# Three changes of place in a hybrid decoder block: the pools of a rows stage, the first loads of the attention mix, and the tiles of the second feed-forward product

## The chip, the cores and the metric

The kernel runs on one core of a Trainium2 chip. The metric is the time of one execution in microseconds of the device. The time before is the median of three runs. One execution was recorded by the hardware profiler, and all lines of a profile come from it. The engines are PE (matrix products), DVE, ACT and POOL (vector work), and SP, which here issues most of the DMAs (POOL issues the stores made with `store`).

## The reference, cut to what matters

One layer on x of 2048 rows by 1024 columns, all in float32:

```python
h = rmsnorm(x, norm_pre_mix)
z = h @ w_in                      # columns: g_u g_v | f_q f_k f_v | f_gate | m_q
out_a = gmlp_spatial_gating(g_u, g_v, w_s, b_s, v_norm)      # 6 groups x 64, chunks of 128
out_b = forgetting_attention(f_q, f_k, f_v, log_sigmoid(f_gate + b_forget))   # 6 heads x 64, causal
out_c = memory_cross_attention(m_q, rmsnorm(mem), w_mem_kv)  # 4 heads x 64, 256 memory rows
x = x + rmsnorm(concat(out_a, out_b, out_c) @ w_out)
f = square(relu(rmsnorm(x) @ w_ff1)) @ w_ff2                 # 1024 -> 4096 -> 1024
x = x + rmsnorm(f)
```

## The kernel before, in words

**Numbers and products.** Every product is made from three matmuls: each operand is split into a high part (a rounded copy, ACT, L195, or `halves` at L399 to L403) and a low part (the difference, mostly DVE, L197), and high x high, high x low and low x high are added in PSUM (`mm3`, L203 to L205). The large products use seven products of blocks in place of eight. Their numbers 1, 7, 2, 6, 4, 5, 3 are in the names of the tiles: m = 7, 5, 6 and 3 are sums and differences of blocks, made by POOL or DVE, the others are blocks themselves. A product of a stage is `product(acc, m, first)`.

**Stages.** The 2048 rows are two halves, s = 0 and 1, of 1024 rows.

1. `rows_stage(s, h)`: loads pairs of 128-row tiles of x (L411), norms them, transposes them on PE (`pt`, L431), makes the halves and the block sums of h, stores h for later use to `bq_d` (L444), and multiplies by the value columns (`va`). The values go to `v_d` (L457) and the forget gates to `gate`. Its SBUF pools are xa, xb, xd, xv and xc, opened in that order, for normed rows, block sums, values, and high and low halves. They are closed at the end of the stage, and the next stage's weight pools take their addresses.
2. The columns stage (`column_weights`, `columns`): the rest of w_in, in column blocks. Raw weights `wr0c`, `wr1c` are loaded, their sums `sc` made, split into `w_c`, and used in the products `fxc`, `fyc`, `fzc`. Results go through split copies (`oh_c`, `ol_c`) to `qhi`, `qlo`, `khi`, `klo` and others in device memory. After the second rows stage `forget_sums` (L476 on) makes the cumulative log-sigmoid; it needs an Exp table on ACT.
3. The attention mix: the scores, softmax and value products of every head (L825, L826, L836, L865, L745 to L767), the gating (`gating`), the memory heads and the output weights' loads are steps of a planner (`Plan`), each with an engine, a cost and an earliest time. Its run gives the order in which instructions are written on every engine. `loads` and `block` in `forgetting` issue the loads of q, of the keys, of the cumulative sums (`cb`) and of the values; `tokens` in `gating` issues the loads of a tile of h (`hr`, two DMAs from `bq_d`), which ACT casts to `ht` and POOL completes, for the gating products `ga`.
4. The output product, its norm, and the norm and block sums for the feed-forward part.
5. The first feed-forward product: for each s, 16 blocks `pr` of 256 columns of w_ff1. Per block POOL makes four sums of weights (`sf`, L289 to L292), ACT and DVE split seven blocks of weights, PE runs seven products, and relu and square on ACT (L1429, L1430) write `hid`, 512 x 512 tiles in device memory. POOL also makes one sum of products per block (`c_f`, L322), which waits for product 5's neighbour `k_f` on ACT. `last_chunk(pr)`, in s = 1 only, does ahead of time what the last chunk of the second product needs: for each of eight units u it loads hidden values (`lr`) at block LATER[u], makes four sums on POOL (`ls`, L1368 to L1371) one block later, and splits them (`lh`) and stores them to `hs_d` (L1401) two blocks later.
6. The second feed-forward product: eight chunks c of 512 rows of w_ff2, each with four pairs of units (s, n, q). `chunk_weights(c)` loads two pieces `w2r` (L1472), makes their eight sums on POOL (L1476 to L1479) and splits them into `w`; `unit` loads the hidden values `hr` (L1504), makes four sums `hs` (`hidden_sums`, L1368 to L1371) and splits them into `hc`. The products `gx`, `gy`, `gz` are added into `ya` in SBUF (L1523, L1525). The loads of the first pieces `w2r0` are issued only after the load of block 10 of w_ff1 (`issue_after(loads["f1_10"])`).

**What sets the order.** Outside the mix, instructions are written in the order in which a scheduler places the code, and the pools decide what a new tile waits for: a tile at an address that earlier tiles used can only be written when their last readers are done. Code in `tc.high_priority()` is placed ahead; `behind(ins)` holds it until an instruction is placed. DMAs of SP leave in the order of its queue, and a wait in SP holds everything behind it.

**Places in SBUF at the boundary of 5 and 6.** `extra` (pool `wox`, on the right side) holds one raw block of the output weights and of s = 0's hidden input, and stays open to the end of the first product. `h2raw` (right) is the raw tile for s = 1's input. After it, before the change, lr (2 tiles), ls (8) and lh (7) are all opened on the right. When the first product ends, `ff_st` closes, and the second product opens its pools, `fraw` for the raw pieces `w2r` among them.

## Time and profile before

| what | value |
| --- | --- |
| time, median of three runs | 2284.72 us (2282.15 to 2287.16) |
| the profiled execution's own time | 2283.18 us |
| its span | 2281.1 us |
| mean granted clock of PE | 0.983 |
| busy: PE, DVE, ACT, POOL | 2173.9, 1632.0, 1354.7, 1029.2 us |
| rows stage s=1 (140 to 192.5): PE busy | 47.74 of 52.50 us |
| attention mix (297 to 833): PE busy | 501.01 of 536.00 us |
| first feed-forward product (1010 to 1640): PE busy | 617.80 of 630.00 us |
| boundary (1640 to 1660): PE busy | 12.40 of 20.00 us |
| second product (1660 to 2255): PE busy | 595.00 of 595.00 us |

A timeline line gives the start, the time of one instruction or of a group (x2, x4), the engine, the line of the kernel, the operation, output <- input, and in brackets the idle time before it with what ended it. The granted clock is the share of full speed that PE's clock had; at 0.50 a matmul takes twice its time.

### The profile page before, as it was taken

The page shows a single profiled execution, that of the slowest core. Times are in us where ns is not written, and L with a number is a line of the kernel's source. Part 1 is how long each engine was busy: PE and PEld are TensorE (multiplying, and loading weights), DVE is VectorE, ACT ScalarE, POOL GpSimd, SP SyncE. Part 2 cuts the span into 40 slices and gives each one's busy share as a digit, 9 for nine tenths or more (in the row PEclk, how much of TensorE's full clock was granted, in tenths as well). Part 3 has the DMA queues.
Part 4 walks back from the last instruction along what each step waited for, and adds up shares of the span by engine and source line. Part 5 has one row for each costly group of instructions (what it writes and reads, how often), then busy time and mean ns, then how long its engine had stood idle before and what let it go on. Part 6 is the DMA issues. An engine that isn't in the chain of part 4 may idle for free. (4 is left out here: it accounts for less than half of the span.)

```text
span 2281.1 us, 33146 instructions
## 1 busy us (share of the span) xinstructions
PE 2173.9 (95%) x10468; PEld 1827.3 (80%) x10468; DVE 1632.0 (72%) x3137; ACT 1354.7 (59%) x2929; POOL 1029.2 (45%) x1073
## 2 busy tenths in 40 slices
PE   8998989999999989998999999999899999999997
PEld 7787778888888867776888878888778888888885
DVE  7776657777877788895333364555678988999888
ACT  6465467878777776665555576666554443444333
POOL 5444433452636255644333334444655345534524
PEclk9999999999999989999999999999999999999998
DMA  7775685365463255785333364555432212221277
GB/s 253 248 241 173 211 226 139 84 165 135 104 153 98 83 180 204 262 293 203 111 111 111 111 212 152 194 193 184 151 111 93 93 56 93 93 92 57 93 248 296
DMA packets 236843, 359.98 MB, mean 158 GB/s; under 512 B 24806, under 2 KB 141420, under 8 KB 235644
## 3 DMA queue, kind: packets, MB, share of 16 engines
q1 hardware_dynamic: 224380, 316.92, 44.1%
q0 software_dynamic: 12288, 40.95, 4.8%
q8 instruction: 83, 1.36, 0.2%
q14 instruction: 92, 0.75, 0.1%
HBM read 232.88 MB, written 124.91 MB: 157 GB/s over the span
## 5 line engine op out<-in xcount | busy, mean ns | idle before, releaser
L205 PE MATMUL fxf<-h,w_f 128*128 128x512 f32 x512 | 201.3, 393 | 4.1 <-DVE w_f L197 4.1
L203 PE MATMUL gx<-w,hc 128*128 128x512 f32 x512 | 199.0, 391 | 6.4 <-DVE ya L1525 5.8
L204 PE MATMUL fxf<-h,w_f 128*128 128x512 f32 x512 | 200.9, 392 | 2.4 <-DVE h L197 2.4
L203 PE MATMUL fxf<-h,w_f 128*128 128x512 f32 x512 | 201.1, 393 | 1.1 <-ACT k_f L317 0.6
L195 ACT ACTIVATE hc<-hs 128x256 fp32r<-128x256 f32 x224 | 93.4, 417 | 179.6 <-PE gx L205 99.2
L204 PE MATMUL gx<-w,hc 128*128 128x512 f32 x512 | 199.7, 390 | 0.0
L205 PE MATMUL gx<-w,hc 128*128 128x512 f32 x512 | 196.4, 390 | 0.0
L197 DVE TENSOR_TENSOR w_f<-sf,w_f 128x512 fp32r<-128x512 f32 x128 | 95.9, 750 | 138.3 <-ACT w_f L195 135.9
L1525 DVE TENSOR_TENSOR ya<-gx,ya 128x512 f32<-128x512 f32 x232 | 156.6, 684 | 43.9 <-PE gx L205 43.2
L753 DVE TENSOR_TENSOR pl<-pt,ph 128x512 fp32r<-128x512 f32 x240 | 140.9, 605 | 46.9 <-ACT ph L749 45.4
L865 ACT ACTIVATE p<-p,nm 128x512 f32<-128x512 f32 (+2 forms) x240 | 156.9, 657 | 24.6 <-DVE nm L855 24.3
L749 ACT CAST ph<-pt 128x512 fp32r<-128x512 f32 x240 | 120.5, 523 | 62.5 <-PE pt L745 55.5
L195 ACT ACTIVATE w_f<-sf 128x512 fp32r<-128x512 f32 x128 | 80.8, 631 | 100.4 <-PE fxf L204 56.9
L197 DVE TENSOR_TENSOR w_f<-wrf,w_f 128x512 fp32r<-128x512 f32 x96 | 75.6, 788 | 88.2 <-ACT w_f L195 88.2
L836 DVE CUSTOM_DVE_ANT_0 p<-s,cb 128x512 f32<-128x512 f32 (+2 forms) x216 | 124.7, 593 | 17.6 <-PE pt L745 9.7
L197 DVE TENSOR_TENSOR hc<-hs,hc 128x256 fp32r<-128x256 f32 x224 | 124.9, 560 | 9.3 <-ACT hc L195 9.1
L195 ACT ACTIVATE hc<-hr 128x256 fp32r<-128x256 f32 x168 | 68.3, 416 | 101.4 <-PE gx L205 64.8
L745 PE MATMUL pt<-ident,p 128*128 128x128 f32 x816 | 123.9, 277 | 2.7 <-ACT p L865 2.7
L815 POOL TENSOR_TENSOR cm<-cb,cmask 128x128 f32<-128x128 f32 x96 | 45.0, 469 | 175.2 <-DVE mx L836 141.5
L745 PEld LDWEIGHTS pt<-ident,p 128*128 128x128 f32 x816 | 102.7, 144 | 22.9 <-ACT p L865 2.9
L203 PEld LDWEIGHTS gx<-w,hc 128*128 128x128 f32 x512 | 96.3, 188 | 28.4 <-DVE ya L1525 7.4
L205 PEld LDWEIGHTS fxf<-h,w_f 128*128 128x128 f32 x512 | 97.1, 190 | 26.0 <-DVE w_f L197 5.7
(389 smaller groups left out, 7066.8 us busy)
## 6 DMA issues: line engine op xcount, KB each, us to landing
wrf<-in_w_ff_dram SPq DMA_DIRECT2D x64, 512.0 KB, 4.8
hid<-c_f SPq DMA_DIRECT2D x128, 256.0 KB, 2.5
hr<-hid SPq DMA_DIRECT2D x56, 512.0 KB, 4.0
w2r<-in_w_ff_dram SPq DMA_DIRECT2D x16, 1024.0 KB, 5.6
b<-ty POOLq DMA_DIRECT2D x56, 256.0 KB, 3.8
hs<-lh SPq DMA_DIRECT2D x56, 256.0 KB, 2.7
hc<-hs SPq DMA_DIRECT2D x56, 256.0 KB, 5.1
xt<-in_x_dram SPq DMA_DIRECT2D x16, 512.0 KB, 4.7
```

The costliest lines, as they stand in the source:

```text
L195: a = nc.scalar.activation(hi, src, AF.Copy, scale=scale)
L197: return a, (eng or nc.vector).tensor_tensor(out=lo, in0=src, in1=f32(hi), op=ALU.subtract)
L203: nc.tensor.matmul(acc, lh, rh, start=first, stop=False, skip_group_check=more)
L204: nc.tensor.matmul(acc, lh, rl, start=False, stop=False, skip_group_check=more)
L205: nc.tensor.matmul(acc, ll, rh, start=False, stop=last, skip_group_check=more)
L745: nc.tensor.transpose(pt[:, a * P : (a + 1) * P], source(a, j), ident)
L749: nc.scalar.copy(hi[:, a0 * P :], tiles["pt", j][:, a0 * P :])
L753: nc.vector.tensor_tensor(out=lo[:, a0 * P :], in0=tiles["pt", j][:, a0 * P :], in1=f32(tiles["hi", j][:, a0 * P :]), op=ALU.subtract,)
L815: nc.gpsimd.tensor_tensor(out=t["cm", i], in0=cc[b][:, qs], in1=cmask, op=ALU.add)
L836: nc.vector.tensor_tensor_reduce(out=pr[:, cols], in0=t["s", a, c][:, cols], in1=sub, scale=1.0, scalar=-3.0e38, op0=ALU.subtract, op1=ALU ...
L865: nc.scalar.activation(pr, pr, AF.Exp, bias=t["nm", a], accum_out=t["rs"][:, a, c : c + 1])
L1525: nc.vector.tensor_tensor(out=y, in0=a, in1=y, op=ALU.add)
```

## The change

Three things are moved. No instruction is added or taken away.

**A, pools of the rows stage.** The pools are opened in the order xa, xd, xc, xb, xv. The sum of their sizes stays, but the weight tiles of the columns stage behind them lie where xd and xc were rather than where xb was.

**B, the start of the mix.** The tile for the gating's tokens is taken where it was, but its two loads are put into a list `held`. They are issued at once only if a key has been loaded already; otherwise when `block` has issued its loads (`token_loads` at its end). The first tile's loads are put behind the first key's second half.

**C, the second product's places.** `extra` is closed after the raw tile of s = 1; `fraw` is opened in its place, before the first product of s = 1 runs; ls has 4 tiles on the left in place of 8 on the right; lh and lr stay on the right. The units of the last chunk are taken from block 0 on.

```diff
@@ rows_stage
             xa = st.enter_context(pool(f"xa{s}", 1))
+            xd = st.enter_context(pool(f"xd{s}", 1))
+            xc = st.enter_context(pool(f"xc{s}", 2))
             xb = st.enter_context(pool(f"xb{s}", 6))
-            xd = st.enter_context(pool(f"xd{s}", 1))
             xv = st.enter_context(pool(f"xv{s}", 4))
-            xc = st.enter_context(pool(f"xc{s}", 2))
@@ load_pair
-            load(t[HD:, :n], lo[r, cols])
+            loads[tag] = nc.sync.dma_start(f32(t[HD:, :n]), lo[r, cols])
@@ forgetting, block
                     load(vv[c], v_d[4 * c : 4 * c + 4, :, h, :].rearrange("i p d -> p i d"))
+                    token_loads()
@@ ahead of gating
+        held = []
+
+        def token_loads():
+
+            while held:
+                t, i = held.pop(0)
+                s, e, q = i // 8, i // 4 % 2, i % 4
+                with behind(*[loads["k"]][: i < 1]):
+                    for k2 in range(2):
+                        nc.sync.dma_start(t[:, k2 * KH : (k2 + 1) * KH], bq_d[s][q][:, ((1, 2), (0, 3))[e][k2]])
@@ gating, tokens
-                        s, e, q = i // 8, i // 4 % 2, i % 4
                         t["hr", i] = xp.tile([P, D], F32, name=f"hr{i}", tag="x").rearrange("p (k t) -> p k t", k=KT)
-                        for k2 in range(2):
-                            nc.sync.dma_start(
-                                t["hr", i][:, k2 * KH : (k2 + 1) * KH], bq_d[s][q][:, ((1, 2), (0, 3))[e][k2]]
-                            )
+                        held.append((t["hr", i], i))
+                        if "k" in loads:
+                            token_loads()
@@ feed-forward part
-    extra = ff_st.enter_context(pool("wox", 1, side="right")), "x"
+    extra_st, down_st = ExitStack(), ExitStack()
+    extra = extra_st.enter_context(pool("wox", 1, side="right")), "x"
...
-        lp, LATER = {}, (1, 3, 4, 6, 7, 9, 10, 12)
+        lp, LATER = {}, (0, 1, 2, 4, 5, 6, 8, 9)
...
-                lp.update({a: st.enter_context(pool(f"l{a}", n, side="right")) for a, n in (("r", 2), ("s", 8), ("h", 7))})
+                extra_st.close()
+                down_raw = down_st.enter_context(pool("fraw", 2, side="right"))
+                lp["s"] = st.enter_context(pool("ls", 4))
+                lp.update({a: st.enter_context(pool(f"l{a}", n, side="right")) for a, n in (("h", 7), ("r", 2))})
...
-    with ExitStack() as st:
+    with down_st as st:
...
-        rp = st.enter_context(pool("fraw", 2, side="right"))
+        rp = down_raw
```

Three places show how the order moves. The first is ACT at the end of the second rows stage, before (-) and after (+): `vs` are the last two values, `w_c` the first column weights' high parts, `ls` the forget sums.

```order
 L195 ACTIVATE vs_2046<-va_2021 128x6x64
 L195 ACTIVATE vs_2076<-va_2051 128x6x64
-L476 ACT_TABLE_LOAD
-L476 ACTIVATE ls<-ls 128x96
 L195 ACTIVATE w_c_0_1_2115<-wr0c_0_2098 128x512
 L195 ACTIVATE w_c_0_7_2133<-sc_0_7_2104 128x512
 L195 ACTIVATE w_c_0_2_2151<-wr1c_0_2099 128x512
 L195 ACTIVATE w_c_0_6_2175<-sc_0_6_2106 128x512
+L476 ACT_TABLE_LOAD
+L476 ACTIVATE ls<-ls 128x96
```

The table load and the Exp of the forget sums moved behind four splits.

The second is SP at the start of the attention mix, first before the change. `cb` is a row of cumulative sums, `hr` the gating's tokens, `v`, `q` and `k` a head's values, queries and keys.

```order
L802 DMA cb_0_3126<-c_d 128x512
L1052 DMA hr_3112<-bq_91 128x512 x2
L189 DMA v_0_3128<-v_d 128x4x128
L802 DMA cb_1_3133<-c_d 128x512
L189 DMA q_0_1_3115<-qhi_67 64x512 x2
L189 DMA q_0_1_3118<-qlo_70 64x512 x2
L189 DMA k_0_3123<-khi_73 64x512
L189 DMA k_0_3123<-klo_76 64x512
```

The same place after the change:

```order
L802 DMA cb_0_3124<-c_d 128x512
L189 DMA v_0_3126<-v_d 128x4x128
L802 DMA cb_1_3133<-c_d 128x512
L189 DMA v_1_3135<-v_d 128x4x128
L802 DMA cb_2_3227<-c_d 128x512
L189 DMA q_0_1_3113<-qhi_67 64x512
L699 DMA q_0_1_3113<-qhi_67 64x512
L189 DMA q_0_1_3116<-qlo_70 64x512
L699 DMA q_0_1_3116<-qlo_70 64x512
L189 DMA k_0_3121<-khi_73 64x512
L699 DMA k_0_3121<-klo_76 64x512
L986 DMA hr_3112<-bq_91 128x512 x2
```

The tokens' two loads moved behind the first key, and one more tile of values and one more row of sums came ahead of it.

The third is POOL in block 12 of the first product in s = 1, where block 13's weight sums `sf` are made; `ls` are sums for the last chunk, `c_f_12` is block 12's sum of products. Before:

```order
L1368 TENSOR_TENSOR ls_7_17252<-lr_17069 128x256
L1369 TENSOR_TENSOR ls_5_17253<-lr_17069 128x256
L289 TENSOR_TENSOR sf_13_7_17446<-wrf_13_17443 128x512
L1370 TENSOR_TENSOR ls_6_17254<-ls_5_17253,lr_17069 128x256
L1371 TENSOR_TENSOR ls_3_17255<-lr_17069,ls_6_17254 128x256
L290 TENSOR_TENSOR sf_13_5_17447<-wrf_13_17443 128x512
L291 TENSOR_TENSOR sf_13_6_17448<-sf_13_5_17447,wrf_13_17443 128x512
L292 TENSOR_TENSOR sf_13_3_17449<-wrf_13_17443,sf_13_6_17448 128x512
L322 TENSOR_TENSOR c_f_12_17404<-k_f_12_17402,k_f_12_17324 128x512
```

And after; L1490 to L1493 are the lines L1476 to L1479 of before, the sums of the first rows of w_ff2:

```order
L1490 TENSOR_TENSOR t_0_7_18031<-w2r_0_18029 128x512
L1490 TENSOR_TENSOR t_1_7_18040<-w2r_1_18038 128x512
L290 TENSOR_TENSOR sf_13_5_17487<-wrf_13_17483 128x512
L1491 TENSOR_TENSOR w2r_0_18029<-w2r_0_18029 128x512
L1491 TENSOR_TENSOR w2r_1_18038<-w2r_1_18038 128x512
L1492 TENSOR_TENSOR t_0_6_18032<-w2r_0_18029 128x512
L291 TENSOR_TENSOR sf_13_6_17488<-sf_13_5_17487,wrf_13_17483 128x512
L1492 TENSOR_TENSOR t_1_6_18041<-w2r_1_18038 128x512
L1493 TENSOR_TENSOR t_0_4_18033<-w2r_0_18029,t_0_6_18032 128x512
L292 TENSOR_TENSOR sf_13_3_17489<-wrf_13_17483,sf_13_6_17488 128x512
L1493 TENSOR_TENSOR t_1_4_18042<-w2r_1_18038,t_1_6_18041 128x512
L322 TENSOR_TENSOR c_f_12_17474<-k_f_12_17472,k_f_12_17394 128x512
```

The eight sums of w2r moved here from the boundary, where they stood behind block 14's `c_f` and among the first `hs` sums; the `ls` sums of unit 6 are gone from this block.

## Prediction

> **What bounds the kernel now.** I read the windows first, then the timelines of the engines around each stretch that the change touches. The page's first line gives the span.
>
> ```profile
> span 2281.1 us, 33146 instructions
> ```
>
> The profiled execution took 2283.18 us, 2.1 more than this span and 1.5 less than the median of 2284.72. My sum is made against 2283.18, and 1.5 is added at the end. The windows below have as columns: length, then busy time and count for PE, PEld, DVE, ACT and POOL, then granted clock, DMA share, GB/s.
>
> ```profile
> 179.50:182.50 3.00, 1.44 (x7) 1.47 (x8) 3.00 (x6) 2.01 (x4) 2.80 (x3) 0.66 0.77 191
> 197.50:200.90 3.40, 3.40 (x9) 2.57 (x9) 3.40 (x7) 0.75 (x2) 1.37 (x1) 0.50 1.10 326
> 299.90:303.30 3.40, 3.11 (x9) 2.42 (x10) 1.64 (x7) 0.65 (x2) 3.34 (x4) 0.50 1.07 343
> 310.10:313.50 3.40, 2.79 (x8) 2.55 (x9) 1.59 (x6) 2.85 (x7) 1.09 (x1) 0.51 1.06 244
> 1566.04:1585.08 19.04, 19.04 (x86) 15.77 (x85) 13.55 (x17) 12.99 (x27) 10.43 (x9) 1.00 0.70 234
> 1640.00:1660.00 20.00, 12.40 (x43) 8.83 (x42) 17.19 (x21) 11.12 (x24) 13.86 (x12) 0.83 0.09 21
> 1644.80:1651.60 6.80, 4.23 (x10) 3.37 (x11) 6.80 (x6) 2.15 (x5) 6.64 (x7) 0.50 0.09 34
> 1660.00:2255.00 595.00, 595.00 (x2626) 492.34 (x2625) 527.60 (x933) 247.71 (x573) 287.07 (x294) 1.00 0.35 119
> ```
>
> The last row says that in the second product PE never waits: 595.00 of 595.00 at full clock. Over most of the program PE is the bound, and the same matmuls are issued before and after. So time can only be won where PE stands idle, and in the half-clock stretches behind such idle time: a stretch of 3.4 us at 0.50 does 1.7 us of full-clock work and costs 1.7. The change touches three such places: the end of the second rows stage (180 to 197), the start of the attention mix (297 to 311), and the boundary between the two feed-forward products (1640 to 1660). A gain there should stay, because PE is full behind it and the later order is unchanged. Differences under 0.2%, or 4.6 us, can hardly be told from no change.
>
> **Part A, the pools of the rows stage.** The same tiles get other addresses, and the next stage's column weights no longer wait for the same readers. In stage s=0 no engine's order changes, so I cost it at nothing. In s=1 PE has these idle times:
>
> ```profile
> 178.85 0.63 PE L431 MATMUL pt<-ident,h 128*128 128x128 f32 x4 [1.13 <-DVE h L399]
> 181.06 1.30 PE L431 MATMUL pt<-ident,h 128*128 128x128 f32 x5 [1.58 <-DVE h L399]
> ...
> 196.74 0.50 PE L203 MATMUL fxc<-hc,w_c 128*128 128x512 f32 x1 [4.24 <-ACT w_c L195]
> ```
>
> The last one waits for ACT's split of the first column weights. On ACT that split stands behind the table load of the forget gate:
>
> ```profile
> 192.54 0.87 ACT L195 ACTIVATE vs<-va 128x384 fp32r<-128x384 f32 x2 [0.94 <-PE va L205]
> 194.59 1.28 ACT L476 ACT_TABLE_LOAD   x1 [1.18 <-issue]
> 195.89 0.28 ACT L476 ACTIVATE ls<-ls 128x96 f32<-128x96 f32 x1
> 196.08 0.61 ACT L195 ACTIVATE w_c<-wr0c 128x512 fp32r<-128x512 f32 x1
> ```
>
> After the change four w_c splits stand directly behind the two vs splits, and the table load behind them. ACT is free of vs at 192.54 + 0.87 = 193.41. Today PE starts 196.74 - 196.08 = 0.66 after the split starts, so it would start at about 194.07: 2.67 us earlier, with an idle time of 4.24 - 2.67 = 1.57 left. What is late next is DVE's low half of the same weights: it now stands ahead of the L477 to L481 chain instead of behind its start, so it is not late. The forget sums move back by four splits. Nothing at the start of the columns stage reads them.
>
> The two idle times at L431 wait for DVE's normalised rows. The tiles' loads move ahead of two stores in SP's queue, and the L399 steps move forward in DVE's order. The most that can go is 1.13 + 1.58 and one half-clock stretch, 4.4 in all. On the other side DVE was busy for the whole of the 3.00 us in the first row of the windows, so moving one step forward moves another back, and the second half of the last weight load now stands behind a store of v_d: I allow a loss of 1.6, one more wait of the longer kind. Because of the full DVE I take 1.3, nearer to nothing than to 4.4. I leave the half-clock stretch at 197.5 where it is, since an idle time of 1.57 remains. Part A: 2.7 + 1.3 = 4.0, from 1.1 to 7.1.
>
> [...]
>
> **Part B, the first keys ahead of the gating's tokens.** PE waits twice here:
>
> ```profile
> 300.19 0.77 PE L825 MATMUL s<-k,q 128*128 128x512 f32 x1 [3.46 <-DMA k<-klo]
> ...
> 310.71 0.77 PE L826 MATMUL s<-k,q 128*128 128x512 f32 x1 [3.19 <-DMA q<-qlo]
> ```
>
> SP issues the loads:
>
> ```profile
> 285.07 0.35 SPq L802 DMA_DIRECT2D cb<-c_d  x1
> 287.83 0.80 SPq L1052 DMA_DIRECT2D hr<-bq  x2
> ...
> 294.08 0.55 SPq L189 DMA_DIRECT2D k<-klo  x1
> ...
> 305.10 0.45 SPq L189 DMA_DIRECT2D q<-qlo  x1
> ```
>
> Before the tokens (hr) SP stands still from 285.42 to 287.83, 2.41 us, until their buffer is free. The first key's second half is issued at 294.08. After the change the tokens go behind the first key, so this stop no longer delays it. But v_1 and cb_2 come ahead of it instead: two transfers of the tokens' size, so the bytes ahead of the key stay the same. The gain at the first wait lies between 0 and 2.41, and I take 1.5: the stop of 2.41 is wholly behind the key in the new order, but four q loads still come first. The second wait ends 310.71 - 305.10 = 5.6 us after the last q load's issue. That load still stands behind the gating weights and four wur loads. PE reaches it 1.5 earlier and waits longer there, up to the whole 1.5. I count half of that back: net 0.7.
>
> The moved tokens are two DMAs. Issued behind the key, at about 294.08 - 1.5 + 0.55 = 293.1, they land by the same 5.6 at 298.7. Work of the scores stands between that and the first gating products on PE. If that cover is gone, ACT waits at the tokens' cast with the first exponentials queued behind it: up to 2 us lost. Part B: 0.7, from -2 to 3. The upper end is the 2.41 and part of the second wait.
>
> **Part C, the places for the second product.** The boundary costs 20.00 - 12.40 = 7.60 us of idle PE, and from 1644.8 PE ran 4.23 us at half clock, 2.1 lost: about 9.7 in all.
>
> ```profile
> 1642.63 0.47 PE L203 MATMUL gy<-w,hc 128*128 128x512 f32 x1 [1.42 <-DVE c_f L322]
> 1642.93 0.40 PE L204 MATMUL gy<-w,hc 128*128 128x512 f32 x1
> 1647.37 0.79 PE L205 MATMUL gy<-w,hc 128*128 128x512 f32 x1 [4.04 <-DVE hc L197]
> ```
>
> Both waits are for DVE, and DVE is slow because POOL works beside it:
>
> ```profile
> 1637.25 2.94 DVE L197 TENSOR_TENSOR w<-w2r,w 128x512 fp32r<-128x512 f32 x2
> 1640.11 1.77 DVE L197 TENSOR_TENSOR w<-t,w 128x512 fp32r<-128x512 f32 x1
> 1641.80 0.68 DVE L322 TENSOR_TENSOR c_f<-fyf,k_f 128x512 f32<-128x512 f32 x1
> 1642.40 0.68 DVE L197 TENSOR_TENSOR w<-t,w 128x512 fp32r<-128x512 f32 x1
> 1643.00 2.90 DVE L197 TENSOR_TENSOR hc<-hr,hc 128x256 fp32r<-128x256 f32 x2
> 1645.83 1.49 DVE L197 TENSOR_TENSOR hc<-hs,hc 128x256 fp32r<-128x256 f32 x1
> ```
>
> The same split of w took 0.68 and 1.77. POOL at that time:
>
> ```profile
> 1632.69 3.00 POOL L1477 TENSOR_TENSOR w2r<-w2r 128x512 f32<-128x512 f32 x2
> 1636.04 0.74 POOL L1368 TENSOR_TENSOR hs<-hr 128x256 f32<-128x256 f32 x1 [0.36 <-DMA hr<-hid]
> 1636.74 1.19 POOL L1369 TENSOR_TENSOR hs<-hr 128x256 f32<-128x256 f32 x1
> 1637.89 3.44 POOL L1478 TENSOR_TENSOR t<-w2r 128x512 f32<-128x512 f32 x2
> ```
>
> After the change w_ff2's first rows are loaded some blocks earlier and their eight sums (L1476 to L1479) stand among block 13's weight sums, away from the boundary. The hidden loads are issued earlier too. DVE's eight steps from 1637.25 to 1647.32 take 10.07 us. At 0.68 each, the price without POOL and an upper one for the 256-wide steps, they take 5.4: at most 4.6 saved. But POOL still has two units of four hidden sums there, whose first waits for PE to give its buffer free, so it cannot move ahead. If each holds a DVE step up by 1.19 - 0.68 = 0.5, that is 4.0 of the 4.6, leaving 0.6. Between these ends I take 3 for the wait of 4.04, because the hidden sums come early in that stretch, and 1 of the 1.42. Nothing of the half-clock loss is counted. Part C: 4.0. Its upper end is 7 (the two waits whole, 5.5, and most of the half-clock loss), its lower end -1: the last sum of block 15 (c_f on POOL) now stands behind ten hidden sums, and its relu on ACT ahead of a split of w that PE needs. Ten sums at 0.74 to 1.19 are 7.4 to 11.9 us, so that chain may end a little after PE's need.
>
> At block 12 the eight sums use POOL's idle time, 19.04 - 10.43 = 8.6 us there, and the four ls sums that move away. Spare POOL time is the cover that makes them free. The second rival prices its loss. The earlier places of the LATER splits are steps of equal number among other blocks with PE full: nothing.
>
> **Sum.** 4.0 + 0.7 + 4.0 = 8.7 us: 2283.18 - 8.7 = 2274.5, and 1.5 more on the scale of the median, 2276.0. All lower ends together (1.1 - 2 - 1) give 2286.6, all upper ends (7.1 + 3 + 7) 2267.6.
>
> **Rivals.** First, the waits are given back: B's second wait takes all of the first, and the new chain POOL c_f, ACT relu, w split takes C's place. Then only A's 2.7 stays, 2282.0. For it: both second waits are in the rows above or in the order. Against it: the eight POOL sums do leave the boundary. Chance 0.20, within 0.2%.
>
> Second, slower: POOL is overfull in block 12.
>
> ```profile
> 1586.44 0.63 ACT L1429 ACTIVATE c_f<-c_f 128x512 f32<-128x512 f32 x1 [1.12 <-POOL c_f L322]
> ```
>
> ACT already waits here for POOL's last sum of the block, with the next splits behind it. Eight sums at 1.50 to 1.72 are 12.0 to 13.8. The four ls sums that leave have at most the row's mean of 10.43 / 9 = 1.16 each, at least half of it: 2.3 to 4.6. So 7.4 to 11.5 come into 8.6 of idle time: it fits, or is 2.9 over. Each sum can also hold DVE up by 1.77 - 0.68 = 1.09, 8.7 together, against DVE's idle 19.04 - 13.55 = 5.5: 3.2 over. A product is 19.04 / 7 = 2.7 us of PE, and the split behind c_f is for a product about three later, so it decides when lateness exceeds roughly 5 us. If both overruns reach PE (6.1) with two half-clock stretches (3.4), A and B's 4.7 are outweighed, and if C gives nothing as well the time is 2284.7 + 4.8 = 2289.5, or 2290. Against it: mostly it fits, and three products cover the rest. Chance 0.08.
>
> Third, more: the clock stays up behind the shortened idle times. Then the stretches at 197.5 and at 310.1 or 299.9 stay full, 2 x 1.7 = 3.4 more: 2272.6. [...] The 0.66 beside 1.13 and 1.58 speaks against it. Chance 0.10.
>
> **How the numbers follow.** The forecast has 0.62, between its own ends mostly 2268 to 2280. Faster: 0.62 + 0.10 = 0.72; within 0.2%: 0.20; slower: 0.08. The range from 2268 to 2286 takes in the forecast's ends nearly whole, the first and the third rival, and leaves out the second.
>
> **What would show it.** In the profile of the changed kernel: A is right if the first fxc of the second columns stage shows about 1.6 of idle in place of 4.24, with the table load behind the splits; the two L431 waits show the 1.3. B is right if the first wait for the key is near 2 and the next one for q grows by less. C is right if PE's idle time from 1630 to 1650 falls from 7.6 to about 3.6 and DVE's splits there are near 0.68, and if no wait appears where blocks 12 and 13 meet. It is wrong if PE waits there, if gaps return as waits for ACT behind c_f, or if the mix shows a wait for the tokens.

## The result, and the profile after

The median after the change is 2268.82 us in seven runs (2261.80 to 2273.54), against 2284.72 us in seven runs of the kernel before. The ratio is 0.9928, 95% interval 0.9913 to 0.9943: faster by 16.4 us, between 13.0 and 19.9. The forecast was 2276.0 in a range from 2268 to 2286. The sign and the places were right, and the range held by 0.8 us at its lower end; the gain is nearly twice the 8.7 of the sum.

The profiled execution of the changed kernel took 2261.80, the lowest of its seven runs. The first lines of its page are the span and PE's busy time:

```profile
span 2260.0 us, 33156 instructions
...
PE 2166.3 (96%) x10468; PEld 1820.0 (81%) x10468; DVE 1646.4 (73%) x3137; ACT 1354.3 (60%) x2929; POOL 1030.5 (46%) x1073
```

Span less busy time is PE's idle time: 2260.0 - 2166.3 = 93.7 us, where before it was 2281.1 - 2173.9 = 107.2. So 13.5 of the 21.1 us between the two spans are idle time that is gone. The count of matmuls is the same, and the busy time fell by 7.6 because PE spent fewer us at half clock: summed over the records, 57.8 us before and 38.9 after. In the trace of before, matmuls of 128 x 512 start 0.427 us apart at a granted clock of 0.50 (1035.16 to 1039.86, eleven steps) and 0.227 at 1.00 (the 2626 of the second product in 595.00 us): 1.88 times as long, and not quite the twice of the section on time and profile before. A microsecond at half clock then costs 1 - 0.227 / 0.427 = 0.47, and the difference of 18.9 is worth 8.9. The matmuls took 1.3 longer otherwise.

The windows of the changed kernel at the places the prediction spoke of (length, busy time and count of PE, PEld, DVE, ACT, POOL, then granted clock, DMA share, GB/s):

```profile
1551.40:1570.50 19.10, 19.10 (x86) 15.81 (x85) 10.70 (x12) 11.61 (x21) 18.38 (x13) 1.00 0.72 235
1626.50:1646.50 20.00, 18.05 (x72) 14.43 (x72) 19.00 (x32) 16.33 (x39) 13.10 (x12) 0.91 0.41 126
1630.40:1633.80 3.40, 3.40 (x10) 2.67 (x9) 3.40 (x5) 3.40 (x10) 2.97 (x4) 0.51 0.11 40
1650.00:2232.00 582.00, 581.85 (x2567) 481.62 (x2566) 518.82 (x909) 240.27 (x552) 280.69 (x286) 1.00 0.34 114
```

The boundary (second row) now has 20.00 - 18.05 = 1.95 us of idle PE where it had 7.60, and the half-clock stretch behind it (third row) is 3.4 us long where it was 6.8. PE is still full behind it (last row), and full in block 12, where POOL is now busy for 18.38 of 19.10 us (first row).

**Place A.** PE's waits at the end of the second rows stage, in the timeline of the changed kernel (start, us, engine, line, operation, then idle time before it and what ended it):

```profile
177.70 0.45 PE L203 MATMUL va<-wv,hc 128*128 128x390 f32 x1 [1.16 <-ACT hc L402]
178.93 2.16 PE L431 MATMUL pt<-ident,h 128*128 128x128 f32 x12 [0.60 <-DVE h L399]
191.44 0.50 PE L203 MATMUL fxc<-hc,w_c 128*128 128x512 f32 x1 [1.13 <-ACT w_c L195]
```

The wait of 4.24 in front of the first column product is 1.13. The two waits of 1.13 and 1.58 for DVE at L431 did not simply shrink: one of 0.60 for DVE is left, and waits for ACT's halves (L402) are new, 1.16 in the first line and 0.35 at 171.13, so 2.11 in all for 2.71. On ACT the splits of the column weights now follow the value splits directly, with the table load behind them:

```profile
190.00 0.87 ACT L195 ACTIVATE vs<-va 128x384 fp32r<-128x384 f32 x2 [0.72 <-PE va L205]
190.75 0.63 ACT L195 ACTIVATE w_c<-wr0c 128x512 fp32r<-128x512 f32 x1
...
192.32 0.63 ACT L195 ACTIVATE w_c<-sc 128x512 fp32r<-128x512 f32 x1
192.96 1.28 ACT L476 ACT_TABLE_LOAD   x1
```

**Place B.** PE's waits at the start of the attention mix:

```profile
291.61 0.48 PE L826 MATMUL s<-k,q 128*128 128x512 f32 x1 [2.60 <-DMA k<-klo]
...
295.41 0.55 PE L826 MATMUL s<-k,q 128*128 128x256 f32 x1 [3.10 <-DMA k<-klo]
...
303.30 0.47 PE L827 MATMUL s<-k,q 128*128 128x512 f32 x1 [0.89 <-DMA q<-qlo]
```

There were two waits, 3.46 for the first key and 3.19 for a q. Now there are three: 2.60 for the first key, 3.10 for the second, 0.89 for the q. Their sum is 6.59, where it was 6.65. SP's loads show why:

```profile
284.90 0.45 SPq L699 DMA_DIRECT2D k<-klo  x1
287.54 1.37 SPq L986 DMA_DIRECT2D hr<-bq  x2
...
289.58 0.55 SPq L699 DMA_DIRECT2D k<-klo  x1
```

SP still stands still before the tokens (hr), from 284.90 + 0.45 = 285.35 to 287.54, 2.2 us. That stop used to lie ahead of the first key and now lies ahead of the second, whose half is issued at 289.58 and used 5.8 us later, at 295.41.

**Place C.** Of four waits at the boundary between the two feed-forward products one is left, and the first products start without a wait:

```profile
1626.58 0.47 PE L203 MATMUL gy<-w,hc 128*128 128x512 f32 x1
...
1629.70 0.50 PE L205 MATMUL gy<-w,hc 128*128 128x512 f32 x1 [1.95 <-DVE hc L197]
```

DVE's splits there, and the sum of products between them:

```profile
1622.64 2.05 DVE L197 TENSOR_TENSOR w<-w2r,w 128x512 fp32r<-128x512 f32 x2 [0.25 <-ACT w L195]
1624.61 1.22 DVE L197 TENSOR_TENSOR w<-t,w 128x512 fp32r<-128x512 f32 x1
1625.75 0.68 DVE L322 TENSOR_TENSOR c_f<-fyf,k_f 128x512 f32<-128x512 f32 x1
1626.36 0.68 DVE L197 TENSOR_TENSOR w<-t,w 128x512 fp32r<-128x512 f32 x1
1626.95 1.83 DVE L197 TENSOR_TENSOR hc<-hr,hc 128x256 fp32r<-128x256 f32 x2
1628.70 1.28 DVE L197 TENSOR_TENSOR hc<-hs,hc 128x256 fp32r<-128x256 f32 x2
```

The same eight steps that took 10.07 us before end with the first of the last pair, at 1629.64: 7.0 us. On POOL the hidden sums alone are left beside them:

```profile
1621.02 0.74 POOL L1379 TENSOR_TENSOR hs<-hr 128x256 f32<-128x256 f32 x1 [11.09 <-PE fxf L204]
1621.72 1.27 POOL L1380 TENSOR_TENSOR hs<-hr 128x256 f32<-128x256 f32 x1
...
1628.58 0.79 POOL L1382 TENSOR_TENSOR hs<-hr,hs 128x256 f32<-128x256 f32 x1
```

**Where the time came from.** For every matmul the two traces give two starts; their difference is the lead of the changed kernel there. It grows from 2.0 at 150 to 6.4 at 204 (A: 4.4), from 7.7 at 280 to 8.7 at 320 (B: 1.0), and from 14.6 at 1600 to 21.2 at 1680 (C: 6.6). That is 12.0 of the 21. The other 9 came where the change moves nothing: 2 at 60, and some more between 204 and 280 and between 320 and 1060. At those places five half-clock stretches of before are missing (6.8 us long at 61.0; 3.4 each at 334.0, 371.6, 610.5 and 863.1), and 6.8 us of others are new: (20.4 - 6.8) x 0.47 = 6.4 of the 9. The experiments show whether that is the change's doing.

### The profile page after: what moved, and what is told of

Same layout as the page of the kernel before. It is cut to its first block, busy times and chain, and to the rows that moved or that the text cites. A ratio compares the mean times of both kernels' runs of the same rounds, so it can differ in the third digit from the quotient of the medians.

```text
span 2260.0 us, 33156 instructions
## 1 busy us (share of the span) xinstructions
PE 2166.3 (96%) x10468; PEld 1820.0 (81%) x10468; DVE 1646.4 (73%) x3137; ACT 1354.3 (60%) x2929; POOL 1030.5 (46%) x1073
## 3 DMA queue, kind: packets, MB, share of 16 engines
q8 instruction: 83, 1.36, 0.3%
## 4 chain that ended last, share of the span: by engine, by line
PE 74%; DVE 8%; DMA 7%; issue 4%; ACT 4%; POOL 2%; SPq 1%; DVEq 0%; POOLq 0%; ACTq 0%
PE gx L205 5%; PE gx L204 5%; PE gx L203 5%; PE fxf L204 5%; PE fxf L203 5%; PE fxf L205 5%; PE pt L745 3%; PE gy L205 2%; PE gy L204 2%; PE gy L203 2%; PE fyf L203 2%; PE fyf L204 2%; PE fyf L205 2%; PE pv L767 2%; PE pv L766 2%
## 5 line engine op out<-in xcount | busy, mean ns | idle before, releaser
L197 DVE TENSOR_TENSOR w_f<-wrf,w_f 128x512 fp32r<-128x512 f32 x96 | 80.8, 841 | 88.4 <-ACT w_f L195 88.4
L1379 POOL TENSOR_TENSOR hs<-hr 128x256 f32<-128x256 f32 x56 | 51.7, 923 | 152.0 <-DMA hr<-hid 79.9
```

The source lines that it names most:

```text
L197: return a, (eng or nc.vector).tensor_tensor(out=lo, in0=src, in1=f32(hi), op=ALU.subtract)
L1379: eng.tensor_tensor(out=sm[7], in0=a11, in1=a21, op=ALU.subtract)
```

## The experiments

Twelve runs were made, one of them the changed kernel once more; none leaves any work out. Each ratio is to the kernel before, run on the same chip. The leads gained at the three places, read as above from each profile against that of before, are kept in one table (A between 150 and 204, B between 280 and 320, C between 1600 and 1680). In brackets are places where that kernel changes nothing.

| kernel | ratio, 95% interval | A | B | C |
|---|---|---|---|---|
| the change, first profile | 0.9928, 0.9913 to 0.9943 | 4.4 | 1.0 | 6.6 |
| after_again | 0.9946, 0.9928 to 0.9963 | 3.3 | 1.5 | 6.6 |
| pools_only | 0.9983, 0.9971 to 0.9994 | 1.5 | (-0.4) | (0.6) |
| keys_only | 0.9996, 0.9983 to 1.0009 | (-2.5) | 0.3 | (1.3) |
| places_only | 0.9965, 0.9955 to 0.9975 | (0.2) | (-0.1) | 6.6 |
| table_later | 0.9986, 0.9976 to 0.9996 | 3.8 | (-1.4) | (-0.1) |
| pools_places | 0.9926, 0.9912 to 0.9940 | 1.7 | (-0.3) | 6.6 |
| sums_held | 0.9925, 0.9911 to 0.9940 | 4.0 | 0.2 | 8.0 |
| old_units | 0.9949, 0.9932 to 0.9965 | 3.0 | 1.6 | 5.1 |
| late_rows | 0.9946, 0.9933 to 0.9958 | 3.3 | 1.7 | 3.6 |
| sums_between | 0.9949, 0.9936 to 0.9961 | 1.5 | 0.6 | 3.6 |
| tokens_second_key | 0.9935, 0.9921 to 0.9950 | 1.6 | 1.0 | 8.2 |
| held_and_second | 0.9941, 0.9927 to 0.9955 | 3.1 | -2.4 | 8.0 |

The brackets say how far one profile can be trusted at a place: up to 2.5 us come and go where nothing is changed, with the half-clock stretches. At C they are within 1.3. The 8.2 of tokens_second_key at C is the same single wait without the half-clock stretch behind it. At B no gain in the table is above 1.7, so none of them stands clear of these differences.

**Each part alone.** The pools of the rows stage on the kernel before:

```diff
             xa = st.enter_context(pool(f"xa{s}", 1))
-            xb = st.enter_context(pool(f"xb{s}", 6))
             xd = st.enter_context(pool(f"xd{s}", 1))
-            xv = st.enter_context(pool(f"xv{s}", 4))
             xc = st.enter_context(pool(f"xc{s}", 2))
+            xb = st.enter_context(pool(f"xb{s}", 6))
+            xv = st.enter_context(pool(f"xv{s}", 4))
```

> Only part A (the order of the pools in the rows stage) on the kernel before. Theory 'own place': A acts at the end of the second rows stage alone, worth 4.4 us in the profile of the whole change (2.0 us ahead at 140 us, 6.4 ahead at 200), so about 2280 where the kernel before takes 2284.7; the first fxc of the second columns stage waits about 1.1 us where it waited 4.2. Rival 'A also carries the rest ahead of the mix': the 2.4 us won at 58 us and the 1.3 won between 236 and 268 come from A as well, so 7.5 to 8.5 us, about 2276.5. Rival 'given back': the start of the mix waits for loads that do not come earlier, so under 2 us remain behind 310 us.

Measured: 2279.80 against 2283.30, faster by 3.9 us by the ratio (1.4 to 6.6). In its profile the waits at the end of the rows stage are:

```profile
192.50 0.50 PE L203 MATMUL fxc<-hc,w_c 128*128 128x512 f32 x1 [1.55 <-ACT w_c L195]
194.76 0.80 PE L205 MATMUL fxc<-hc,w_c 128*128 128x512 f32 x1 [1.00 <-DVE w_c L197]
```

The first is 1.55 where the prediction had 1.57. But a new wait of 1.00 follows, for DVE's low half of the same weights, which the prediction had called not late, and behind the two PE ran at half clock:

```profile
193.80:200.60 6.80, 5.84 (x14) 4.60 (x15) 6.52 (x15) 2.87 (x5) 1.46 (x2) 0.50 1.01 300
```

The lead went from 0.4 at 150 to 1.6 at 190 (1.2 around L431) and 4.2 at 194 (the split: 2.7), and fell back to 1.8 at 204. Both terms of A are there in size; this profile lost 2.4 of them in the stretch. Of the 1.2 the waits give 0.5: 0.62 for DVE and 0.46 and 1.16 for ACT stand where 1.13 and 1.58 for DVE stood. The rest fits the half-clock stretch of before at 180.4, which is not there in this profile.

What made DVE's low half late stands right ahead of it, a step of the forget sums that took 0.26 us before the change. DVE, then POOL in pools_only:

```profile
192.78 1.32 DVE L475 SCALAR_TENSOR_TENSOR ls<-gate 128x96 f32<-128x96 f32 x1
194.02 0.68 DVE L197 TENSOR_TENSOR w_c<-wr0c,w_c 128x512 fp32r<-128x512 f32 x1
```

```profile
192.70 1.28 POOL L403 TENSOR_TENSOR hc<-t,hc 128x512 fp32r<-128x512 f32 x1
```

The step began 0.08 us into a sum of POOL and ended 0.12 behind it. Of the ten profiles with A, nine have this step at 1.31 to 1.33 us, begun 0.07 to 0.10 into that sum, and in the same nine PE waited 1.00 or 1.01. In the tenth, the first profile of the change, it began 0.89 into the sum and took 0.50, and PE did not wait.

The first keys ahead of the tokens, on the kernel before:

```diff
+            loads[tag] = nc.sync.dma_start(f32(t[HD:, :n]), lo[r, cols])
...
+                    token_loads()
...
+                        held.append((t["hr", i], i))
+                        if "k" in loads:
+                            token_loads()
```

> Only part B (the first keys ahead of the gating's tokens) on the kernel before. Theory 'own place': one microsecond or less, 2283.5 to 2285; the waits at the first key and at the second q load are still there, the first one shorter than 3.5. Rival 'B also carries the mix': the 3.1 us won between 334 and 380 us and the 2 won by 620 in the profile of the whole change come from the other order of loads, so 4 to 6 us, about 2279.5. Rival: tokens late, a wait for the tokens' cast, slower by 1 to 3 us.

Measured: 2282.08 against 2283.30, ratio 0.9996 (0.9983 to 1.0009): no difference that can be told. Its waits are 2.21 for the first key, 3.90 for the second and 1.29 for the q, 7.40 in all where there were 6.65; the gain at the first key is given back at the second.

The places of the second product, on the kernel before:

```diff
-        lp, LATER = {}, (1, 3, 4, 6, 7, 9, 10, 12)
+        lp, LATER = {}, (0, 1, 2, 4, 5, 6, 8, 9)
...
+                extra_st.close()
+                down_raw = down_st.enter_context(pool("fraw", 2, side="right"))
+                lp["s"] = st.enter_context(pool("ls", 4))
...
```

> Only part C (places of the second product, units from block 0 on) on the kernel before. Theory 'own place': 6.6 us at the boundary between the two feed-forward products as in the profile of the whole change (14.6 ahead at 1640 us, 21.2 at 1680), so about 2278; PE's idle time there about 2 in place of 7.6 and no wait in blocks 12 to 14. Rival 'chance of the clock': of the 6.6 about 1.7 is a half-clock stretch that falls otherwise in other runs, so 4 to 5 us, about 2280.

Measured: 2276.03 against 2283.30, faster by 8.0 us by the ratio (5.7 to 10.3). C is the largest part, about twice its 4.0. The boundary looks as in the changed kernel to 0.01 us (one wait of 1.96), and the lead grows by the same 6.6. The three parts alone sum to 3.9 + 0.9 + 8.0 = 12.8 us.

**The order alone for A.** On the kernel before, only the Exp of the forget sums, and with it the table load, is held behind the split of a column weight; the addresses stay:

```diff
-                split(w[m][0], w[m][1], of[m])
+                marks["w", nm, m] = split(w[m][0], w[m][1], of[m])[0]
...
-        nc.scalar.activation(e, t, AF.Exp)
+        with behind(marks["w", "c1_0", 6]):
+            nc.scalar.activation(e, t, AF.Exp)
```

> The kernel before, with the pools as they were, and only the forget gate's Exp (and so its table load) held behind the fourth split of the first column weights; DVE's steps behind the Exp move with it, nothing else moves. Theory 'order': the gain of A at the first fxc is the table load's place alone, so PE waits there about 1.6 us or less in place of 4.2 and the time falls by 2.7, plus up to 1.7 if the half-clock stretch goes: 2280.3 to 2282. Rival 'address': the split cannot be written before POOL's last readers of the old tiles are done, so it waits for POOL instead, and the fxc wait stays at 3 us or more: 2283.5 to 2285. In both the two waits at L431 (1.1 and 1.6) stay, and what pools_only wins beyond this kernel is theirs.

Measured: 2279.41 against 2283.30, faster by 3.2 us by the ratio (0.9 to 5.5). PE's waits in its profile:

```profile
177.09 0.63 PE L431 MATMUL pt<-ident,h 128*128 128x128 f32 x4 [1.24 <-DVE h L399]
179.30 1.79 PE L431 MATMUL pt<-ident,h 128*128 128x128 f32 x8 [1.59 <-DVE h L399]
192.52 0.50 PE L203 MATMUL fxc<-hc,w_c 128*128 128x512 f32 x1 [1.48 <-ACT w_c L195]
```

The L431 waits stay as they were, and the 4.24 falls to 1.48. So the 2.7 of A is the place of the table load in ACT's order, with DVE's steps behind the Exp that move along, and needs no new address. What the addresses change besides are the waits around L431 and the wait of 1.00 for DVE's low half, which does not appear here: the step of the forget sums took 0.26. No half-clock stretch follows either: the granted clock is 1.00 from 192.50 to 199.30.

**The change again.** The same file measured a second time, without an edit, to see what two profiles of one kernel differ by.

> The changed kernel once more, beside three variants of it. Theory 'sum of parts': the single parts gave 3.9, 0.9 and 8.0 us on their own, 12.8 together, so about 0.9944 of the kernel before, and the 21 us of its first profile were a lucky execution: the stretches at 58, 236 to 268 and 334 to 380 us, where nothing was changed, fall otherwise this time. Rival 'they help each other': 0.9928 again, 16 us, because the shorter half-clock stretches only go when all waits ahead of the mix go.

Measured: 2271.12 against 2283.11, faster by 12.3 us (8.4 to 16.4). The profiled execution took 2279.14, the highest of its six runs. Its three places gained 3.3 + 1.5 + 6.6 = 11.4. But between 320 and 1600 it fell back by 6.9 (lead 5.6 to -1.3), where the first profile gained 5.9 over the same matmuls. So the 9 us outside the three places in the first profile are not steady: this one lost 6 us there. That nothing outside the places comes from the change is not shown by this. In all nine kernels that hold A and C, the gain by the ratio is above the sum of the places in the profile, by 0.9 to 8.6 us. A's waits in this profile, and then a window behind the first of them:

```profile
191.85 0.50 PE L203 MATMUL fxc<-hc,w_c 128*128 128x512 f32 x1 [1.54 <-ACT w_c L195]
194.10 0.50 PE L205 MATMUL fxc<-hc,w_c 128*128 128x512 f32 x1 [1.00 <-DVE w_c L197]
```

```profile
192.00:199.00 7.00, 6.00 (x25) 4.44 (x26) 6.69 (x16) 4.03 (x7) 2.03 (x3) 1.00 0.99 297
```

The waits are those of pools_only to 0.01 us, and here the clock (1.00 in the window's row) stayed up.

**Without B.** The changed kernel with the tokens loaded where they were before, so A and C alone:

```diff
-                    token_loads()
...
-                        held.append((t["hr", i], i))
-                        if "k" in loads:
-                            token_loads()
+                        for k2 in range(2):
+                            nc.sync.dma_start(
+                                t["hr", i][:, k2 * KH : (k2 + 1) * KH], bq_d[s][q][:, ((1, 2), (0, 3))[e][k2]]
+                            )
```

> Parts A and C without B. Singly they gave 3.9 and 8.0 us. Theory 'sum of parts': 11.9 us, 0.9948 of the kernel before, and B adds about a microsecond in the whole change too. Rival 'B works only with A': A's earlier end is given back at the start of the mix while the first key is late (in pools_only 1.8 us ahead at 200 us became 0.4 at 320), so A and C without B give 8 to 9 us.

Measured: 2268.25 against 2285.03, ratio 0.9926 (0.9912 to 0.9940). Nothing is lost without B: the time does not tell B from zero. The gain by the ratio, 16.9 us, is above the 11.9 that was expected from A and C alone, and the interval leaves 0.9948 out; why is open.

**The tokens behind the second key.** The changed kernel with only SP's order changed:

```diff
-                    token_loads()
+                    if c:
+                        token_loads()
...
+            loads.setdefault("t", loads["k"])
...
-                with behind(*[loads["k"]][: i < 1]):
+                with behind(*[loads["t"]][: i < 1]):
```

> The changed kernel with the tokens' two loads behind the second key's loads in place of the first key's; nothing else moves. In the changed kernel PE waits 3.1 us for the second key's second half, issued at 289.6 behind the tokens. Theory: that load leaves 1.5 us earlier, the wait falls to about 1.6 and the time by up to 1.5. Rival 'given back': the tokens come 1.1 us later and PE waits for the gating products or for the next q load instead, no gain.

Measured: 2269.00 against 2283.11, ratio 0.9935 (0.9921 to 0.9950). PE's waits in its profile:

```profile
294.95 0.47 PE L827 MATMUL s<-k,q 128*128 128x512 f32 x1 [1.72 <-issue]
296.57 0.55 PE L827 MATMUL s<-k,q 128*128 128x256 f32 x1 [0.92 <-DMA k<-klo]
307.55 0.47 PE L828 MATMUL s<-k,q 128*128 128x512 f32 x1 [2.99 <-DMA q<-qlo]
```

The second key's 3.10 falls to 0.92, so it was the tokens ahead of it, with SP's stop, that held it. The q's wait grows from 0.89 to 2.99. In both orders the long wait stands at the next key or q behind the tokens.

**What makes C.** Four edits of the changed kernel separate the eight w2r sums, their place on POOL, and the early loads. The intervals of all four overlap those of the two measurements of the change, so what they say is read at the place and not from the time. There the boundary of the changed kernel came out at 6.6 in four profiles, and at 8.2 in one without the half-clock stretch. First, the eight sums held behind block 14's `c_f` on POOL, so that they stand closer to the boundary:

```diff
+                with behind(*[marks["f1_14", 1, 1]][: c < 1]):
                     nc.gpsimd.tensor_tensor(out=t[7], in0=b22, in1=b12, op=ALU.subtract)
...
```

> The changed kernel with the eight sums of the first w_ff2 rows held behind block 14's c_f on POOL, so at the boundary again as in the kernel before, but with their rows long loaded. All other engines as in the changed kernel. Theory 'beside DVE' (the prediction's): sums on POOL beside DVE's splits slow them down, so most of part C goes again, 4 us or more slower than the changed kernel. Rival 'late loads': in the kernel before the sums began late because w2r landed late; with the rows there they run from c_f at once, ahead of DVE's splits at the boundary, and at most 1.5 us are lost. The start and end of the sums on POOL and the wait at gy L205 tell which.

Measured: 2266.68 against 2283.11, ratio 0.9925 (0.9911 to 0.9940). POOL's rows:

```profile
1617.08 2.54 POOL L1491 TENSOR_TENSOR t<-w2r 128x512 f32<-128x512 f32 x2
...
1628.90 1.27 POOL L1379 TENSOR_TENSOR hs<-hr 128x256 f32<-128x256 f32 x1
```

The loss of 4 us that was expected first did not come; the rival did. The eight sums run from 1617.08 to 1628.90, about where POOL of the changed kernel stood idle for 11.09 us just ahead of the boundary, and C is worth 8.0: two waits of 0.84 and 0.83 and no half-clock stretch. Against the change's 1.95 that is only 0.28 less idle time, so most of the 1.4 above 6.6 is the missing stretch. The place in block 12 is not needed; it is enough that the sums end before the splits of DVE on which PE waits begin, here at 1629.83.

Second, the units of the last chunk at their old blocks, meant to make POOL fuller in block 12:

```diff
-        lp, LATER = {}, (0, 1, 2, 4, 5, 6, 8, 9)
+        lp, LATER = {}, (1, 3, 4, 6, 7, 9, 10, 12)
```

> The changed kernel with the units of the last chunk at the blocks of before (1, 3, 4, 6, 7, 9, 10, 12), so that POOL has the four ls sums of a unit in block 12 beside the eight sums of w2r. Theory 'POOL has room': the earlier units are not needed, and the time is the changed kernel's within 1 us. Rival 'overfull' (the prediction's second rival): ACT waits longer for c_f of block 12, PE waits in block 13, 3 to 8 us slower than the changed kernel.

Measured: 2273.19 against 2283.11, ratio 0.9949 (0.9932 to 0.9965). The edit did not do what it was for. The order came out with the eight sums behind block 14's `c_f`, so block 12 was not overfull, and the run tells nothing about that. One sum stayed among the first hidden sums (at 1629.99, 1.74 us), the boundary had waits of 0.53 and 2.95, and C fell to 5.1.

Third, the changed kernel with the first rows of w_ff2 loaded late, behind a store of the hidden values of block 14:

```diff
-                with tc.issue_after(loads["f1_10"].ins) if c == 0 else ExitStack():
+                with tc.issue_after(loads["hid", 1, 14, 1, 0].ins) if c == 0 else ExitStack():
```

> The changed kernel with the loads of the first w_ff2 rows held back to where they stood before the change, behind the store of a result of block 14; the hidden values hr stay early. sums_held lost nothing, so the sums' place on POOL behind block 14 does no harm if the rows are there. Theory 'late loads': with the rows landing some 6 us behind block 14 the eight sums run again until after the first hs sums are due, beside DVE's splits; the wait at gy L205 grows to 3.5 us or more and 3 to 6 us of part C are lost (ratio to the kernel before 0.996 to 0.997). Rival 'late hidden values': in the kernel before it was hr that came late (its first sum waited for it), and with hr early nothing is lost.

Measured: 2272.54 against 2285.03, ratio 0.9946 (0.9933 to 0.9958). POOL's first and last sum:

```profile
1622.83 1.78 POOL L1490 TENSOR_TENSOR t<-w2r 128x512 f32<-128x512 f32 x1 [4.12 <-DMA w2r<-in_w_ff_dram]
...
1636.29 1.79 POOL L1493 TENSOR_TENSOR t<-w2r,t 128x512 f32<-128x512 f32 x1
```

The sums wait for their rows and run into DVE's splits; the waits are 1.11 and 2.94, the half-clock stretch is 6.8 long again, and C is worth 3.6. The early load of the rows is what lets the sums leave.

Fourth, everything loaded early as in the change, but the last four sums put among the hidden sums, as before the change:

```diff
+                with behind(*[marks["f1_14", 1, 1]][: c < 1]):
                     nc.gpsimd.tensor_tensor(out=t[7], in0=b22, in1=b12, op=ALU.subtract)
                     nc.gpsimd.tensor_tensor(out=b12, in0=b12, in1=b11, op=ALU.subtract)
...
+                    with tc.high_priority(), behind(marks["hs5"]):
+                        while waiting:
+                            waiting.pop(0)()
```

> The changed kernel with rows and hidden values loaded early, but the last four of the eight sums held on POOL until behind the second hs sum, among the hs sums as in the kernel before; PE, ACT and DVE then follow the order of the kernel before at the boundary. If POOL's sums beside DVE are what costs, early loads do not help: splits of 1.2 to 1.8 us on DVE, a wait at gy L205 of 3 us or more, 3 to 5 us slower than the changed kernel. If only late loads cost, within 1.5 us of it.

Measured: 2273.18 against 2285.03, ratio 0.9949 (0.9936 to 0.9961). POOL at the boundary, then DVE, then PE:

```profile
1631.14 3.44 POOL L1497 TENSOR_TENSOR t<-w2r 128x512 f32<-128x512 f32 x2
...
1635.68 3.19 POOL L1498 TENSOR_TENSOR t<-w2r,t 128x512 f32<-128x512 f32 x2
```

```profile
1630.84 2.60 DVE L197 TENSOR_TENSOR w<-w2r,w 128x512 fp32r<-128x512 f32 x2 [0.26 <-ACT w L195]
1633.36 1.77 DVE L197 TENSOR_TENSOR w<-t,w 128x512 fp32r<-128x512 f32 x1
...
1636.25 2.90 DVE L197 TENSOR_TENSOR hc<-hr,hc 128x256 fp32r<-128x256 f32 x2
```

```profile
1635.88 0.47 PE L203 MATMUL gy<-w,hc 128*128 128x512 f32 x1 [1.08 <-DVE c_f L322]
...
1640.08 0.79 PE L205 MATMUL gy<-w,hc 128*128 128x512 f32 x1 [3.50 <-DVE hc L197]
```

Four sums beside DVE bring back splits of 1.77 and a pair of 2.90, and waits of 1.08 and 3.50, close to the 1.42 and 4.04 of before. C falls from 6.6 to 3.6, so the sums beside DVE are worth 3.0 of it, and the other 3.6 stay without them: the two later waits of before do not return but for 0.17 us. Nor do they in late_rows and old_units, so they hang neither on the early rows of w_ff2 nor on the units' blocks. What is left is the early loads of the hidden values and the order on ACT, where four splits of hidden values stand ahead of the relu of `c_f` also in sums_between and not in the kernel before. No run takes these two apart.

**A try at more.** The two edits that shortened waits, together:

```diff
+                with behind(*[marks["f1_14", 1, 1]][: c < 1]):
                     nc.gpsimd.tensor_tensor(out=t[7], in0=b22, in1=b12, op=ALU.subtract)
...
-                with behind(*[loads["k"]][: i < 1]):
+                with behind(*[loads["t"]][: i < 1]):
```

> Both variants that lost nothing together: sums held behind block 14's c_f, tokens behind the second key. At the boundary 8.0 us ahead of the kernel before where the change is 6.6, at the start of the mix a microsecond ahead of the change: 2 to 2.5 us better than the changed kernel if the half-clock stretches fall alike, 0.992 to 0.9935 of the kernel before. Rival: not to be told from it.

Measured: 2271.80 against 2285.03, ratio 0.9941 (0.9927 to 0.9955). C has its 8.0, and 2.4 went at B in a profile with 10.2 us of half clock there. PE's waits at B are 2.99, 0.85 and 3.38 us, where the same order of loads had 1.72, 0.92 and 2.99 in tokens_second_key, so the first of them is not steady. The expected 0.992 to 0.9935 was missed by the ratio, though not by its interval. The intervals of this kernel, of sums_held and of the change overlap: no version clearly beats the change.

## Why the prediction was right, and where its size was off

**What was assumed throughout held.** PE is the bound behind the boundary (581.85 of 582.00 us), and the lead of 21.2 us at 1680 is still 21.2 at 2200. The forecast of 8.7 stands beside 12.3 and 16.4 in two measurements of the change, 12.0 and 11.4 read from the three places, and 12.8 as the sum of the parts alone.

**A, forecast 4.0, measured 3.9 alone, 4.4 and 3.3 in two profiles of the change.** The 2.7 of the table load is shown by the order alone (table_later: the wait falls from 4.24 to 1.48, 2.76). The 1.3 at L431 is one of two outcomes: between 150 and 190 the lead grew by 1.0 to 1.4 us in five of the ten profiles with A and by 0.0 to 0.3 in the other five. Four of these five have a wait of 1.33 to 1.53 for another of ACT's halves (L402) in front, and the first profile of the change has a half-clock stretch at 179.8; against that its wait for the split came out at 1.13 and not at 1.57. One step was wrong: "What is late next is DVE's low half of the same weights ... so it is not late". In nine of the ten profiles PE waited 1.00 for just that, because the step ahead of it on DVE, begun 0.07 to 0.10 us into a sum of POOL, took 1.31 to 1.33 us where it had taken 0.26. Leaving the stretch at 197.5 as a loss was also one of two outcomes: four of the ten have one there (pools_only, pools_places, tokens_second_key, sums_between), 6.8 us long where it was 3.4, and six do not.

**B, forecast 0.7, measured 0.9 alone with an interval around zero.** The size fits by luck, for the path was another. The first wait fell by 0.9 in the first profile (1.5 was forecast), and the next wait for a q did not grow but fell from 3.19 to 0.89. What took the gain back was a wait that the prediction had not named, for the second key, because the stop before the tokens now lies ahead of it. tokens_second_key shows this: past the second key, the wait moves on to the q. DMAs were busy all this time, with a share of 1.04 in this window of the changed kernel:

```profile
285.00:304.00 19.00, 11.73 (x47) 9.22 (x46) 7.91 (x28) 9.85 (x22) 9.80 (x18) 0.82 1.04 317
```

That the bytes, and not the order, set the sum of these waits fits this share, and so does the sum itself: 5.4 to 7.4 us in the nine profiles with B, 6.5 to 6.9 in the five without. It was not tried by taking bytes away.

**C, forecast 4.0, measured 6.6 at the place: the term that was mis-sized.** The mechanism was right, POOL's sums beside DVE's splits, and sums_between shows it with 3.0 us. The wait of 4.04 gave less than forecast, 4.04 - 1.95 = 2.1 and not 3, since beside the hidden sums DVE's pair of w still took 2.05, where two at 0.68 are 1.36, and its pair of hc 1.83, where one at 1642.55 took 0.75. The rest was counted too low. The wait of 1.42 went whole and not for 1. The two later waits, 7.60 - 1.42 - 4.04 = 2.1, were counted at nothing and went too. Before the change they were:

```profile
1653.94 0.50 PE L203 MATMUL gx<-w,hc 128*128 128x512 f32 x1 [0.69 <-ACT c_f L1429]
1658.40 0.50 PE L203 MATMUL gy<-w,hc 128*128 128x512 f32 x1 [1.45 <-ACT hc L195]
```

"Nothing of the half-clock loss is counted" left out about 1: the stretch went from 2.1 us lost to 1.7 by the rows, and 0.6 more has no row of its own and stays unexplained. So 2.1 + 1.4 + 2.1 + 1.0 = 6.6. The step that failed is the reading of the boundary as the two waits for which rows were shown. The later ones waited for ACT (a relu of `c_f` and a split of hc) and not for DVE beside POOL. They went with the rest of part C, by the early hidden values or by ACT's order, which is open.

**The rivals.** The first, waits given back, came true for B alone: for A a part of it came at DVE's low half, for C nothing did, and no wait for ACT behind `c_f` appeared at the boundary. The second, POOL overfull in block 12, was near in its cause and absent in its effect: POOL was busy for 18.38 of 19.10 us, and ACT waited 2.40 for its last sum where it had waited 1.12:

```profile
1572.85 0.63 ACT L1440 ACTIVATE c_f<-c_f 128x512 f32<-128x512 f32 x1 [2.40 <-POOL c_f L322]
```

PE was busy for all of the 19.10: a lateness of 1.3 is below the 5 from which that rival decides. The third, the clock staying up, came in part: at the boundary the stretch is 3.4 and not 6.8 long (and gone in sums_held), at A it is a matter of the execution, and at B 6.8 us of it are there as before.

**What stays open.** The measured gain of 16.4 in the first comparison and 12.3 in the second agree within their intervals. Whether the 4 us between them are more than the half-clock stretches of different executions was not settled, nor whether a part of the gain comes from outside the three places.

## What to carry to other kernels

Where PE waits for a split at the start of a stage, look first at what stands ahead of that split on its engine and is not urgent: moving one table load was worth 2.7 us without touching an address. At a boundary count every wait, not only the longest, and see that sums on POOL end before DVE's splits begin: here a split that began inside a sum took up to 1.78 us in place of 0.68. At the start of the mix, with a DMA share of 1.04, a load moved ahead only chose which of the next loads was late (the second key's wait fell from 3.10 to 0.92, the q's grew from 0.89 to 2.99); read the wait of the one behind it before counting a gain.

## What the runs showed of the hardware

The granted clock was read from its records in two traces, that of before and that of the changed kernel. They hold 15 and 10 stretches at half clock. Within each trace the starts of all stretches, and the ends of all but the one that runs to the end of the span, lie whole multiples of 3.41 us apart. Cut at that distance, from the first record to the end, the two traces give 1283 pieces at full clock and 37 at half clock. The 25 full-clock pieces with half clock behind them hold 1.42 us or more of idle PE each, the other 1258 at most 1.75, so between these two both happened. Of the half-clock pieces, the 14 with half clock behind them hold 0.73 us or more, the 23 with full clock behind them at most 0.66. Counted from the start of the span, the changes lie 2.95 us past a multiple of 3.41 in before and 2.29 in the changed kernel. These are counts of two executions and no rule for others.

The end of the second rows stage shows how fine this is. pools_only and after_again have the same two waits there, 1.55 and 1.00 in the one, 1.54 and 1.00 in the other. Behind the first of them the granted clock was 0.50 for 6.8 us in pools_only (193.80 to 200.60) and 1.00 in after_again (192.00 to 199.00). What made the difference was not shown.

In the trace of before, between 1010 and 2200 us, DVE's split of 128 x 512 took 0.67 to 0.69 us in the 265 cases where no sum of POOL was under way when it began, and up to 1.78 in the 70 others. All 70 ended 0.54 to 0.67 us behind the sum, 51 of them 0.55: by the ends of these rows the split waited for the sum rather than running slowly beside it. The split at 1640.11 ends at 1641.88 and POOL's pair at 1637.89 + 3.44 = 1641.33, 0.55 earlier. In sums_between the split of 1.77 us ends at 1633.36 + 1.77 = 1635.13, and POOL's pair of sums at 1631.14 + 3.44 = 1634.58, again 0.55 earlier. So what these splits lost hung on how much of the sum was still to come, up to 1.78 - 0.68 = 1.10 us. In the trace of the changed kernel it was once the other way round: a sum at 1640.94 took 2.95 us, and the two splits of 128 x 512 that began within it took 0.68 each. The sum of products (`c_f`), which reads PE's output as one operand, took 0.68 to 0.69 in the 15 cases in before in which it began inside a sum of POOL.
